# Three gate products and the neighbourhood values as seven half-size products, moved behind the global attention

## The chip, the cores and the metric

The kernel runs on one core of one Trainium2 chip. The metric is the device time of one execution in microseconds (us); the number compared is the median of a few runs of the same program. One execution was also recorded by the hardware profiler. Engines are named as in the profile: PE is TensorE (its matmuls), PEld its weight loads, DVE is VectorE, ACT is ScalarE, POOL is GpSimd, SP the engine that issues most of the DMAs. L185 means line 185 of the kernel.

## The reference

One encoder layer on 512 tokens of 2048 features, in fp32. What the change touches:

```python
proj = h @ w_in[l]                    # 2048 x 8704
qa, ka, va, qb, kb, vb, ga, gb = jnp.split(proj, offs, axis=-1)
...
ya = global_gqa(qa, ka, va)           # 8 heads, 2 key heads, all 512 keys
yb = neighbourhood_attention(qb, kb, vb, nat_rpb[l])   # 8 heads, 8 x 16 windows
merged = jax.nn.sigmoid(ga) * (ya @ w_oa[l]) + jax.nn.sigmoid(gb) * (yb @ w_ob[l])
x = x + g1 * (merged @ w_out[l])
```

Before it, `mod = SiLU(c) @ w_ada + b_ada` gives six vectors of 2048 (shift, scale and gate of the two sub-layers); behind it come an RMS norm, a SwiGLU of width 5632 and a final norm.

## The kernel before

Every product is made three times, from a high and a low half of each operand: `split` (L161 to L165) copies a tile to fp32r on ACT (hi, L163) and subtracts it from the source on DVE (lo, L165), and `mm3` (L180 to L185) issues hi times hi, hi times lo and lo times hi into the same PSUM bank. Weights come as 512 KB pieces: `unit` (L187) loads one into one of 4 `raw` buffers from SP's queue, `wsplit` (L193) splits it into one of 3 `whl` buffers. Later stages add 1 `raw` and 2 `whl` buffers from the pool `wq` (`buffer`, L131).

Two loops use them. `form1` (L230) keeps weights stationary and streams the 512 tokens: two banks of 128 output columns, four pieces, 96 matmuls of 512 columns for a contraction over 2048. `form2` (L248) keeps tokens stationary and streams 512 weight columns: four banks, eight pieces, 192 matmuls. After each piece both call `pump` (L210), which carries on background work: callbacks that are due (`soon`), one of the list `later`, and `pace["steps"]` steps of the generators in `bg`.

The stages around the change, in program order:

- Global attention, `att_a` (L701), four heads, the last four columns of gate A, four heads more (L725 to L733). Its results go to DRAM (`y_d`).
- The pool `p_w` is made and the eight generators of `ada_mod` and `ada_gate` go to `bg` (L736 to L740): 128 steps, each of which loads 512 KB of `w_ada` from POOL's queue into one of three `mw` buffers and adds it, times a column of `c`, to an accumulator on DVE (L357, L335). Four groups of 16 steps make shift2 and scale2, two make gate1, two make gate2. Gate B, columns 0 to 1023 (`gates(sg_b, GB, 0, 8)`, L741): four `form1`.
- Neighbourhood attention (L799 to L808): for each half of the heads the values by `form2` (L801), then for each pair of heads queries and keys by `form1` and two calls of `att_b` (L747): scores, softmax, transposes, values.
- Gate B, columns 1024 to 2047 (L820): four `form1`; through `later` each piece also loads one head's attention result and splits it (`attended`, L814).
- For each pair of output columns one `form1` with `w_oa` and one with `w_ob` (L853 to L857), both over 8 heads; `gated` (L840) multiplies by the sigmoid gate; sum and split give `mT` (L858 to L865). `paces` (L852) gives one or two `ada` steps for each piece.
- `w_out` (L949 to L958): columns 0 and 1 for all tokens, columns 2 and 3 for the first half, then, after a norm of that half, for the second.
- The up and gate products of the SwiGLU by `group7` (L1054): a product of 2 x 2 blocks with seven block products in place of eight (Strassen's scheme in Winograd's form). `wforms` (L998) loads two pieces, makes four sums of quarters on DVE (L1008 to L1011) and splits four tiles; `xforms` has made the same for the features. A step of 512 features is 84 matmuls of 256 columns, four steps a group; then L1080 to L1090 add the banks up.

The order of instructions on each engine is fixed when the program is built, by a list scheduler that takes the first ready instruction by program order in its own model of time; on the chip each engine runs its list in order. Matmuls of a later product so come to stand between the steps of a softmax.

Of the kernel before, what the change touches and what calls it, by code (L numbers as in the profile page):

```python
# [54 lines left out]
MERGED = stream_order(T)  # L55
LAST = MERGED[stream_order(T // 2)]
# [56 lines left out]
def encoder_block(ctx: ExitStack, tc, xp, xT, c, ada1_w, ada2_w, b_ada, norm1_w, w_in, q_norm_w, k_norm_w, bias,  # L113
# [92 lines left out]
    pace = {"steps": 1}  # L206

    paces = []

    def pump():  # L210
        if paces:
            pace["steps"] = paces.pop(0)
# [6 lines left out]
        for _ in range(pace["steps"]):  # L219
            advance()  # L220

    def advance():
        if bg:
            try:
                next(bg[0])
            except StopIteration:
                bg.pop(0)
                advance()

    def form1(ws, c0, g, xs, banks, evac, eng=V):  # L230
# [17 lines left out]
    def form2(w, c0, xs, evac, r0=0, eng=V, tiles=range(NT), tags=("mm",) * NT):  # L248
# [309 lines left out]
    for k1 in range(1, KT + 1):  # L558
# [19 lines left out]
        for c0, accs, ends in GROUPS:  # L578
# [8 lines left out]
            for i, acc in enumerate(accs):  # L587
                sl = slice(i * P, (i + 1) * P)
                b = bank(next(turn))
                for k in range(a0, k1):  # L590
# [3 lines left out]
                    else:  # L594
                        mm3(b, wh[:, sl], wl[:, sl], hh, hl, k == a0, k == k1 - 1, T)
# [17 lines left out]
    def gates(dst, base, j0, j1, eng=V):  # L613
        for j in range(j0, j1, 2):
            form1([w_in], base + j * P, 2, hT, [[bank("mm"), bank("mm")]], keep_gate(dst[j:]), eng)


    p_a = tc.alloc_tile_pool(name="p_a", bufs=1, side="right")
    behind(nc.sync.dma_start(rp, rope.rearrange("p (i s d) -> p i s d", i=NT, s=2)))
    nw = {}  # L620
    for nm, w in (("q", q_norm_w), ("k", k_norm_w)):
        nw[nm] = small.tile([P, HD], F32, tag=f"nw{nm}", name=f"nw{nm}", bufs=1)
        nc.sync.dma_start(nw[nm], w.partition_broadcast(P).rearrange("p o d -> p (o d)"))

    def head_ssq(src, nh, acc):
        for h in range(nh):
            junk = io.tile([P, 512], F32, tag="io", name="junk")[:, :HD]
            S.activation(junk, src[:, h * HD:(h + 1) * HD], AF.Square, accum_out=acc[:, h:h + 1])

    def norm_rope(src, nh, i, r, w, dst):  # L630

        n = nh * HD
        h3 = lambda a: a[:, :n].rearrange("p (h d) -> p h d", h=nh)
        bt = lambda a: a.unsqueeze(1).to_broadcast([P, nh, a.shape[1]])
        a, b, rot = (p_a.tile([P, 512], F32, tag="rt", name="rt", bufs=3) for _ in range(3))
        for h in range(nh):
            hs = slice(h * HD, (h + 1) * HD)
            V.scalar_tensor_tensor(b[:, hs], src[:, hs], r[:, h:h + 1], w, op0=ALU.mult, op1=ALU.mult)
        V.tensor_mul(h3(a), h3(b), bt(rp[:, i, 0, :]))
        for e in range(2):  # L640
            V.tensor_mul(h3(rot)[:, :, e::2], h3(b)[:, :, 1 - e::2], bt(rp[:, i, 1, e::2]))
        V.tensor_add(a[:, :n], a[:, :n], rot[:, :n])
        tp = bank("T")
        for h in range(nh):
            nc.tensor.transpose(tp[:, h * P:(h + 1) * P], a[:, h * HD:(h + 1) * HD], ident)
        hi, lo = (d.rearrange("p (h t) -> p h t", h=nh)[:, :, i * P:(i + 1) * P] for d in dst)
        split(hi, lo, h3(tp))

    kT = pair(p_a, "k", 2 * T, 1)

    def rstds(srcs, nh):
        ssq = small.tile([P, 16], F32, tag="ssq16", name="ssq16")[:, :NT * nh]
        for i, src in enumerate(srcs):
            head_ssq(src, nh, ssq[:, nh * i:nh * i + nh])
        r = rsqrt_mean(ssq, HD, NT * nh)
        return [r[:, nh * i:nh * i + nh] for i in range(NT)]

    def normed(srcs, nh, w, dst):
        rs = rstds(srcs, nh)
        for i, r in enumerate(rs):  # L660
            norm_rope(srcs[i], nh, i, r, w, dst)
            yield

    def values():
        for i in range(NT):
            v = st(F32R)
            vA.append((v[:, :256], v[:, 256:]))
            split(*vA[i], kv[i][:, 256:])
            if i % 2:
                yield  # L670

    vA = []
    q = pair(p_a, "q", 4 * T, 1)
    bg.extend([normed(kv, 2, nw["k"], kT), normed(q_acc, 4, nw["q"], q), values()])
    q1 = [st(F32) for _ in range(NT)]
    form2(w_in, QA + 512, hT, lambda i, b: S.activation(q1[i], b, AF.Copy))
    while bg or soon:
        pump()

    y_d = [dram.tile([P, T], F32, name=f"y{h}") for h in range(16)]  # L680

    def keep_y(h, yb):
        o = aside.tile([P, T], F32, tag="y", name="yo")
        S.activation(o.rearrange("p (h e i) -> p h e i", e=2, i=P), apart(yb), AF.Copy)
        nc.scalar.dma_start(y_d[h], o)

    def softmax(pool, src, scale, w, bufs=2):

        mx = small.tile([P, 1], F32, tag="mx", name="mx")
        V.reduce_max(mx, src, axis=AX.X)  # L690
        V.tensor_scalar(mx, mx, -scale, None, op0=ALU.mult)
        e = pool.tile([P, 512], F32, tag="e", name="e", bufs=bufs)[:, :w]
# [8 lines left out]
    def att_a(h, q, j, kv):  # L701
        kh, kl = (t[:, kv * T:(kv + 1) * T] for t in kT)
        vs = slice(kv * HD, (kv + 1) * HD)
        pts = []
        for i in range(NT):
            if i % 2 == 0:
                pts.append(pair(p_a, "pt", 2 * T, 3))
            sl = slice(j * T + i * P, j * T + (i + 1) * P)
            sc = bank("S")
            mm3(sc, q[0][:, sl], q[1][:, sl], kh, kl, True, True, T)  # L710
            e = softmax(p_a, sc, SCALE, T)
            tp = bank("T")
            for k in range(NT):
                nc.tensor.transpose(tp[:, k * P:(k + 1) * P], e[:, k * P:(k + 1) * P], ident)
            hi, lo = (t.rearrange("p (k q) -> p k q", k=NT)[:, :, i % 2 * P:(i % 2 + 1) * P] for t in pts[-1])
            split(hi, lo, tp.rearrange("p (k q) -> p k q", k=NT))
        yb = bank("Y")
        for n, pt in enumerate(pts):
            ys = yb[:, n * 256:(n + 1) * 256]
            for k in range(NT):  # L720
                ks = slice(k * 256, (k + 1) * 256)
                mm3(ys, vA[k][0][:, vs], vA[k][1][:, vs], pt[0][:, ks], pt[1][:, ks], k == 0, k == NT - 1, 256)
        keep_y(h, yb)

    for h in range(4):  # L725
        att_a(h, q, h, 0)
    q = pair(p_a, "q", 4 * T, 1)
    bg.append(normed(q1, 4, nw["q"], q))
    gates(sg_a, GA, 12, 16)
    while bg or soon:  # L730
        pump()
    for h in range(4):
        att_a(4 + h, q, h, 1)  # L733
    p_a.release()
    p_q.release()
    p_w = tc.alloc_tile_pool(name="p_w", bufs=1, side="right")  # L736
    mod["pool"] = p_w
# [771 lines left out]
```

## Time and profile before

| | |
|---|---|
| median of 3 runs | 2490.66 us (2487.54 to 2491.2) |
| the profiled execution | 2481.72 us, span 2480.0 us |
| granted TensorE clock in it | 0.999 |
| PE busy | 2449.8 us, 16607 matmuls |
| DVE busy | 1883.9 us |
| ACT busy | 1027.6 us |
| moved by DMA | 457.46 MB, 184 GB/s over the span |

A row of the view by windows gives, for a stretch of the span, each engine's busy time with the number of its instructions, the granted clock, the mean busy share of the 16 DMA engines and what they moved. A row of the waits names who waited, for whom, for how long in total, how many times, and the longest. A row of a tile or a line gives shortest, median and longest duration in ns and the first and last start. Matmuls are pipelined: a record of 275 ns does not mean that the next one starts 275 ns later, so the cost of a matmul is read from how many of them fit into a stretch.

### The profile page before, as it was taken

The page shows a single profiled execution, that of the slowest core. Times are in us where ns is not written, and L with a number is a line of the kernel's source. Part 1 is how long each engine was busy: PE and PEld are TensorE (multiplying, and loading weights), DVE is VectorE, ACT ScalarE, POOL GpSimd, SP SyncE. Part 2 cuts the span into 40 slices and gives each one's busy share as a digit, 9 for nine tenths or more (in the row PEclk, how much of TensorE's full clock was granted, in tenths as well). Part 3 has the DMA queues.
Part 4 walks back from the last instruction along what each step waited for, and adds up shares of the span by engine and source line. Part 5 has one row for each costly group of instructions (what it writes and reads, how often), then busy time and mean ns, then how long its engine had stood idle before and what let it go on. Part 6 is the DMA issues. An engine that isn't in the chain of part 4 may idle for free.

```text
span 2480.0 us, 40653 instructions
## 1 busy us (share of the span) xinstructions
PE 2449.8 (99%) x16607; PEld 2270.1 (92%) x16607; DVE 1883.9 (76%) x2511; ACT 1027.6 (41%) x1424; POOL 151.0 (6%) x254
## 2 busy tenths in 40 slices
PE   8999999999999999999999999999999999999998
PEld 7888888888888888888999999999999998999997
DVE  8995776556566577566898888888888885787877
ACT  5223544224334333236744444444444454434333
POOL 0100000111011111011000000000000000000010
PEclk9999999999999999999999999999999999999999
DMA  9864234865655877676353343433433456547563
GB/s 362 296 245 156 81 102 135 273 203 184 191 187 195 300 252 264 233 266 229 111 170 117 122 130 127 136 125 112 132 128 129 135 187 227 190 141 242 192 243 127
DMA packets 217466, 457.46 MB, mean 184 GB/s; under 512 B 15056, under 2 KB 68672, under 8 KB 208832
## 3 DMA queue, kind: packets, MB, share of 16 engines
q1 hardware_dynamic: 179872, 308.19, 37.6%
q0 software_dynamic: 29728, 132.20, 15.2%
q10 hardware_dynamic: 7680, 14.48, 1.6%
q8 instruction: 130, 2.13, 0.3%
q14 instruction: 56, 0.46, 0.1%
HBM read 410.74 MB, written 44.07 MB: 183 GB/s over the span
## 4 chain that ended last, share of the span: by engine, by line
PE 82%; DVE 9%; DMA 4%; issue 2%; ACT 1%; DVEq 0%; POOL 0%; ACTq 0%; POOLq 0%
PE mm L185 18%; PE mm L184 18%; PE mm L183 17%; PE S L183 6%; PE S L184 6%; PE S L185 6%; PE Y L183 3%; PE Y L184 3%; PE Y L185 3%; DVE raw L492 2%; DVE whl L165 2%; DMA raw<-in_w_down 1%; DMA yr<-y 1%; PE T L185 1%; PE T L183 1%
## 5 line engine op out<-in xcount | busy, mean ns | idle before, releaser
L163 ACT ACTIVATE whl<-raw 128x1024 fp32r<-128x1024 f32 (+1 forms) x483 | 462.0, 960 | 758.5 <-PE mm L185 376.5
L165 DVE TENSOR_TENSOR whl<-raw,whl 128x1024 fp32r<-128x1024 f32 (+1 forms) x483 | 531.2, 1109 | 255.5 <-ACT whl L163 255.1
L165 DVE TENSOR_TENSOR whl<-ta,whl 128x1024 fp32r<-128x1024 f32 x104 | 127.2, 1223 | 66.4 <-ACT whl L163 66.4
L357 DVE SCALAR_TENSOR_TENSOR acc<-mw,cact,acc 128x1024 f32<-128x1024 f32 x124 | 158.4, 1278 | 18.8 <-DMA mw<-in_ada_w 14.0
L163 ACT ACTIVATE whl<-tb 128x1024 fp32r<-128x1024 f32 x104 | 110.4, 1061 | 149.6 <-PE S L185 120.1
L163 ACT ACTIVATE whl<-ta 128x1024 fp32r<-128x1024 f32 x104 | 110.1, 1059 | 144.8 <-PE mm L185 113.9
L165 DVE TENSOR_TENSOR whl<-tb,whl 128x1024 fp32r<-128x1024 f32 x104 | 127.0, 1221 | 4.6 <-ACT whl L163 3.6
L335 POOL DMA_DIRECT2D mw<-in_ada_w x112 | 59.8, 534 | 681.7 <-DVE acc L357 384.1
L1008 DVE TENSOR_TENSOR ta<-raw 128x512 f32<-128x512 f32 x104 | 71.8, 690 | 31.5 <-DMA raw<-in_w_down 29.3
L1009 DVE TENSOR_TENSOR ta<-raw,ta 128x512 f32<-128x512 f32 x104 | 71.6, 688 | 28.0 <-DMA raw<-in_w_down 24.9
L183 PE MATMUL mm<-x56h,whl 128*128 128x256 f32 x336 | 92.4, 275 | 0.0
L184 PE MATMUL mm<-x56l,whl 128*128 128x256 f32 x336 | 92.4, 275 | 0.0
L185 PE MATMUL mm<-x56h,whl 128*128 128x256 f32 x336 | 92.4, 275 | 0.0
L183 PE MATMUL mm<-whl,s 128*128 128x256 f32 x320 | 88.1, 275 | 0.0
L183 PE MATMUL mm<-x3h,whl 128*128 128x256 f32 x320 | 88.0, 275 | 0.0
L184 PE MATMUL mm<-x3l,whl 128*128 128x256 f32 x320 | 88.0, 275 | 0.0
L185 PE MATMUL mm<-x3h,whl 128*128 128x256 f32 x320 | 88.0, 275 | 0.0
L183 PE MATMUL S<-x56h,whl 128*128 128x256 f32 x320 | 88.0, 275 | 0.0
L184 PE MATMUL S<-x56l,whl 128*128 128x256 f32 x320 | 88.0, 275 | 0.0
L185 PE MATMUL S<-x56h,whl 128*128 128x256 f32 x320 | 88.0, 275 | 0.0
L184 PE MATMUL mm<-whl,s 128*128 128x256 f32 x320 | 88.0, 275 | 0.0
L185 PE MATMUL mm<-whl,s 128*128 128x256 f32 x320 | 88.0, 275 | 0.0
(1603 smaller groups left out, 8574.4 us busy)
## 6 DMA issues: line engine op xcount, KB each, us to landing
raw<-in_w_in SPq DMA_DIRECT2D x133, 512.0 KB, 4.4
mw<-in_ada_w POOLq DMA_DIRECT2D x112, 512.0 KB, 4.9
raw<-in_w_gate SPq DMA_DIRECT2D x92, 512.0 KB, 3.6
raw<-in_w_up SPq DMA_DIRECT2D x88, 512.0 KB, 3.6
raw<-in_w_down SPq DMA_DIRECT2D x88, 512.0 KB, 5.2
raw<-in_ada_w POOLq DMA_DIRECT2D x29, 1024.0 KB, 7.0
raw<-in_w_out SPq DMA_DIRECT2D x48, 512.0 KB, 5.1
ffd<-c SPq DMA_DIRECT2D x10, 1024.0 KB, 4.8
```

The costliest lines, as they stand in the source:

```text
L163: high = pin(S.activation(hi, src, AF.Copy))
L165: latest[:] = [high, pin(eng.tensor_sub(lo, src, hi))]
L183: nc.tensor.matmul(o, lh, rh, start=start, stop=False, **kw)
L184: nc.tensor.matmul(o, lh, rl, start=False, stop=False, **kw)
L185: nc.tensor.matmul(o, ll, rh, start=False, stop=stop, **kw)
L335: mod["queue"].dma_start(w, ada2_w[n * P:(n + 1) * P, :])
L357: behind(V.scalar_tensor_tensor(acc, part, cact[:, k:k + 1], acc, op0=ALU.mult, op1=ALU.add))
L492: V.scalar_tensor_tensor(raw, raw, 1.0, call, op0=ALU.mult, op1=ALU.mult, accum_out=y)
L1008: V.tensor_sub(t1, b12, b11)
L1009: V.tensor_sub(t2_, b22, t1)
```

## The change

- Gate B's first 512 columns stay plain, right behind the global attention (two `form1`). Their `pump` calls run `FORMS`: for each 512 features, POOL adds hi and lo back to the whole feature (16 additions of 128x512), then DVE makes four sums and two splits (`feature_forms`).
- Gate B's other 1536 columns become three calls of `group7`, and the neighbourhood values two (`by_tokens`: tokens stationary). The pool `p_o` gives them 1 `raw` and 1 `whl` buffer more than the first 4 and 3. The values go to DRAM (`v_d`) and are loaded and split again per half of the heads.
- Only behind that is `p_w` made. The 128 `ada` steps (now the list `mods`) are paced by `slot`: called twice per piece of `form1` and `form2` and twice per head in `att_b`, it adds a rate (0.85 in the neighbourhood attention, 0.72 in `w_oa` and in five of the eight column groups of `w_ob`, 0.6 and 0.5 in `w_out`) and makes a step when the sum reaches 1. At most 96 steps run before `w_out`; the rest load from SP's queue there.
- Behind the last keys the global attention's results are loaded and split into the memory of the features, ahead of the last two heads. Then `w_oa` runs for all columns, its gated results stay in `oa`, and `w_ob` follows for all columns, with the neighbourhood results loaded during `w_oa` and 1 `raw` and 2 `whl` buffers more.
- Products of 512 columns stream as two blocks of 256 (`mm3(..., 256)` in place of `T`), and the host's orders of the tokens change with it.

The core of the diff (`half`, `ORDER`, `wforms` and the rest of the seven-product functions move up unchanged):

```diff
+    def slot():
+        pace["due"] += pace["rate"]
+        if pace["due"] >= 1 and (fetched or mod["next"] < mod["end"]):
+            pace["due"] -= 1
+            advance(mods)
...
-                        mm3(bs[j], hi[:, kk, sl], lo[:, kk, sl], xh, xl, k0 + kk == 0, k0 + kk == n - 1, T)
+                        mm3(bs[j], hi[:, kk, sl], lo[:, kk, sl], xh, xl, k0 + kk == 0, k0 + kk == n - 1, 256)
+                    if kk == m // 2 - 1:
+                        slot()
...
-    def group7(wsrc, xs, order, dst, first_group=False):
+    def group7(wsrc, xs, order, dst, first_group=False, by_tokens=False):
...
+                            if by_tokens:
+                                mm3(o, xh[at], xl[at], wh[:, q], wl[:, q], first, last, 256, skip_group_check=True)
+                            else:
+                                mm3(o, wh[at], wl[at], xh[:, q], xl[:, q], first, last, 256, skip_group_check=True)
+            pump()
...
+    def whole_features(s):
...
+        for k in range(4):
+            G.tensor_add(f[:, k * 512:(k + 1) * 512], *hT[4 * s + k])
+        whole.append(f)
+
+    def feature_forms(s):
...
+        V.tensor_add(sa0, a21, a22)
+        V.tensor_sub(sa1, sa0, a11)
+        V.tensor_sub(sb0, a11, a21)
+        V.tensor_sub(sb1, a12, sa1)
...
+        for src, rs in ((sa, (5, 6)), (sb, (7, 3))):
+            hl = pair(p_o[0], f"s{s}{rs[0]}", 1024, 1)
+            split(*hl, src)
...
+    FORMS = [None, None, wf(0), wf(1), ff(0), wf(2), ff(1), ff(2), wf(3), ff(3)]
+    later.extend(f or (lambda: None) for f in FORMS)
+    gates(sg_b, GB, 0, 4)
+    wq = p_o[0]
+    more_buffers(1, 1)
...
+        group7(lambda s: wforms(w_in, 4 * s, GB + n * 512), hs, range(4), dst)
+        S.activation(c[0], c[0], AF.Sigmoid)
...
+        group7(lambda s: wforms(w_in, 4 * s, VB + hh * 512), hs, range(4), lambda: d, by_tokens=True)
+        nc.scalar.dma_start(v_d[hh], v)
...
+    for n in range(1, 4):
+        gates7(n)
+    for hh in range(2):
+        values7(hh)
...
-    mod["pool"] = p_w
-    bg.extend(ada_mod(k, (s2, b_sc2, n2, t2, b_sh2)) for k in range(0, KT, 4))
+    mod.update(pool=p_w, end=96)
+    mods.extend(ada_mod(k, (s2, b_sc2, n2, t2, b_sh2)) for k in range(0, KT, 4))
...
-    gates(sg_b, GB, 0, 8)
...
-        form2(w_in, VB + half * 512, hT, lambda i, b: split(*v[i], b))
...
+        if hp == 3:
+            p_h.release()
+            p_m = tc.alloc_tile_pool(name="p_m", bufs=1, side="left")
...
+            for h in range(8):
+                attended(ya[h], h, raw_tile("yr")[:, :T])
+        for j in range(2):
+            att_b(h0 + j, qs[j], ks[j], v, slice((hp % 2 * 2 + j) * HD, (hp % 2 * 2 + j + 1) * HD))
...
-    gates(sg_b, GB, 8, KT)
...
+    for j in range(0, KT, 2):
+        tag = next(turn)
+        form1([w_oa], j * P, 2, ya, [[bank(tag), bank(tag)]], gated(sg_a[j:], lambda e: oa[j // 2][:, e * 512:(e + 1) * 512]))
...
+        form1([w_ob], j * P, 2, yT, [[bank(tag), bank(tag)]], gated(sg_b[j:], lambda e: o[e]))
```

More of the change, by code (lines that the diff above doesn't have):

```diff
@@ L611, in keep_gate, with gates @@
         return evac
-    def gates(dst, base, j0, j1, eng=V):
+    def gates(dst, base, j0, j1):
         for j in range(j0, j1, 2):
[L615 to L680, printed above, removed]
@@ L701, in att_a @@
[L701 to L736, printed above, removed]
-    mod["pool"] = p_w
-    bg.extend(ada_mod(k, (s2, b_sc2, n2, t2, b_sh2)) for k in range(0, KT, 4))
-    g1_d, g2_d = ([dram.tile([1, 512], F32, name=f"g{n}d{q}") for q in range(4)] for n in (1, 2))
@@ L866, in encoder_block @@
-    p_y.release()
-    p_w.release()
-    aside.release()
-    taken.update({t: -1 - taken[t] for t in ("raw", "whl")})
-    wq = tc.alloc_tile_pool(name="wq", bufs=1, side="right", reuse_waits="tile")
-    x2_d = dram.tile([T, D], F32, name="x2d")
-    p_w = tc.alloc_tile_pool(name="p_w2", bufs=1, side="left", reuse_waits="tile")
-    mod.update(pool=p_w, queue=nc.sync, end=128)
-    p_r = tc.alloc_tile_pool(name="p_r", bufs=1, side="right", reuse_waits="tile")
-    gate = p_r.tile([P, D], F32, name="gate1")
@@ new lines, in values @@
+    def values():
+        for i in range(NT):
+            v = st(F32R)
+            vA.append((v[:, :256], v[:, 256:]))
+            split(*vA[i], kv[i][:, 256:])
+            if i % 2:
+                yield
+    vA = []
+    q = pair(p_a, "q", 4 * T, 1)
+    bg.extend([normed(kv, 2, nw["k"], kT), normed(q_acc, 4, nw["q"], q), values()])
+    q1 = [st(F32) for _ in range(NT)]
+    form2(w_in, QA + 512, hT, lambda i, b: S.activation(q1[i], b, AF.Copy))
+    flush()
+    y_d = [dram.tile([P, T], F32, name=f"y{h}") for h in range(16)]
@@ new lines, in encoder_block, with __init__, __getitem__ @@
+    for h in range(4):
+        att_a(h, q, h, 0)
+    q = pair(p_a, "q", 4 * T, 1)
+    bg.append(normed(q1, 4, nw["q"], q))
+    gates(sg_a, GA, 12, 16)
+    flush()
+    for h in range(4):
+        att_a(4 + h, q, h, 1)
+    p_a.release()
+    p_q.release()
+    p_o = []
+    quarters = lambda t: t.rearrange("p (a t q n) -> p a t q n", a=2, t=2, q=2)
+    class Cut:
+        def __init__(self, tiles, t):
+            self.tiles, self.t0 = tiles, t * 256
+        def __getitem__(self, ix):
+            c = ix[2] if len(ix) > 2 else slice(0, 256)
+            return self.tiles[ix[1]][:, self.t0 + c.start:self.t0 + c.stop]
@@ new lines, in encoder_block @@
+    for j in range(0, KT, 2):
+        pace["rate"] = 0.72 if j < 10 else 0.0
+        o = [p_y.tile([P, T], F32, tag="o", name="o", bufs=4) for _ in range(2)]
+        tag = next(turn)
+        form1([w_ob], j * P, 2, yT, [[bank(tag), bank(tag)]], gated(sg_b[j:], lambda e: o[e]))
+        for e in range(2):
+            V.tensor_add(o[e], o[e], oa[j // 2][:, e * 512:(e + 1) * 512])
+        mx.append(pair(p_m, f"m{j // 2}", 1024, 1))
+        for e in range(2):
+            mT.append(tuple(Tokens(half(t)[:, :, e]) for t in mx[-1]))
+            (mh, ml), o3 = (t.t for t in mT[-1]), o[e].rearrange("p (t n) -> p t n", t=2)
+            if j + 2 < KT:
+                split(mh, ml, o3)
+            else:
+                V.tensor_copy(mh, o3)
+                V.tensor_sub(ml, o3, mh)
@@ new lines, in encoder_block @@
+    wq = None
+    p_y.release()
+    p_w.release()
+    aside.release()
+    more_buffers(1, 2)
+    wq = tc.alloc_tile_pool(name="wq", bufs=1, side="right", reuse_waits="tile")
+    x2_d = dram.tile([T, D], F32, name="x2d")
+    p_w = tc.alloc_tile_pool(name="p_w2", bufs=1, side="left", reuse_waits="tile")
+    mod.update(pool=p_w, queue=nc.sync, end=128)
+    p_r = tc.alloc_tile_pool(name="p_r", bufs=1, side="right", reuse_waits="tile")
+    gate = p_r.tile([P, D], F32, name="gate1")
+    xc = {cc: p_r.tile([P, NT, 512], F32, tag=f"x{cc}", name=f"x{cc}") for cc in (3, 2)}
@@ new lines, in encoder_block, with load_x @@
+    xn = [None, None, xc[2], p_r.tile([P, NT, 512], F32, tag="n3", name="n3")]
+    xc.update({cc: p_r.tile([P, NT, 512], F32, tag=f"x{cc}", name=f"x{cc}") for cc in (0, 1)})
+    xn[:2] = xc[0], xc[1]
+    sq2 = [small.tile([P, 4], F32, tag=f"sq{i}", name=f"sq{i}", bufs=1) for i in range(NT)]
+    x3d = xp.rearrange("(i p) d -> p i d", p=P)
+    def load_x(cc):
+        if cc == 0:
+            rows(gate, g1_d)
+        nc.sync.dma_start(xc[cc], x3d[:, :, cc * 512:(cc + 1) * 512])
+    for cc in range(4):
+        later.extend([lambda: None] * (2 if cc == 0 else 3))
+        later.append(functools.partial(load_x, cc))
```

514 lines of the change are left out of this document (299 added, 215 removed).

## The prediction

> **What bounds the kernel now.** First the page: who is busy, and who ends the chain of waits.
>
> ```profile
> span 2480.0 us, 40653 instructions
> ...
> PE 2449.8 (99%) x16607; PEld 2270.1 (92%) x16607; DVE 1883.9 (76%) x2511; ACT 1027.6 (41%) x1424; POOL 151.0 (6%) x254
> ...
> PE 82%; DVE 9%; DMA 4%; issue 2%; ACT 1%; DVEq 0%; POOL 0%; ACTq 0%; POOLq 0%
> ```
>
> TensorE is busy nearly throughout. Next, windows by stage: gate B's first half, neighbourhood attention, gate B's second half, `w_oa` with `w_ob`, three stretches of `w_out`; last, 600 us of `group7`. Columns: stretch, its length, busy us (instructions) of PE, PEld, DVE, ACT, POOL, clock, DMA share, GB/s.
>
> ```profile
> 413.00:496.00 83.00, 82.68 (x384) 71.99 (x383) 42.19 (x36) 23.04 (x26) 11.78 (x23) 1.00 0.85 282
> 496.00:778.00 282.00, 280.90 (x1398) 240.84 (x1397) 174.57 (x250) 103.14 (x194) 32.70 (x58) 1.00 0.56 179
> 778.00:861.00 83.00, 81.31 (x375) 70.19 (x374) 53.90 (x57) 31.64 (x42) 14.12 (x25) 1.00 0.92 314
> 861.00:1026.00 165.00, 165.00 (x766) 144.33 (x765) 117.16 (x136) 48.72 (x60) 18.93 (x35) 1.00 0.71 242
> 1026.00:1109.00 83.00, 83.00 (x386) 72.66 (x385) 49.52 (x46) 24.47 (x34) 12.87 (x12) 1.00 0.81 280
> 1109.00:1150.00 41.00, 41.00 (x192) 35.76 (x191) 25.13 (x25) 19.62 (x26) 8.06 (x6) 1.00 0.71 230
> 1300.00:1900.00 600.00, 600.00 (x5375) 600.00 (x5375) 515.50 (x640) 264.98 (x281) 0.00 (x0) 1.00 0.39 127
> ```
>
> Two prices follow. Between 861 and 1026 all matmuls have 512 columns: 165/766 = 215.4 ns each. From 1300 to 1900 all have 256: 600/5375 = 111.6 ns. Streaming in blocks of 512 (first row) or of 256 (fifth) gives the same 215 ns, so `T` to 256 costs nothing. What PE waited for between 395 and 1200 us:
>
> ```profile
> PE mm L185 <- DVE whl L165: 1.9, 3, 0.9
> PE T L778 <- ACT e L770: 1.0, 3, 0.3
> ```
>
> So there is hardly a wait to remove. The change must win by fewer matmuls, and loses whatever new waits it makes.
>
> **The product saving.** Five products of 512 tokens, 512 columns and 2048 features change. Plain: 16 x 4 x 3 = 192 matmuls of 512 columns, 192 x 215.4 = 41.4 us. Sevenfold: 4 steps x 84 = 336 of 256 columns, 336 x 111.6 = 37.5 us. Saved 3.9 us each, 5 x 3.86 = **19.3 us**. It is not an eighth (5.2 us), because two half matmuls cost 223 ns where one whole costs 215: about 8 ns of each matmul do not shrink with its columns.
>
> [...] In `group7` weight loads are busy 600 of 600 us and the spacing is still 111.6 ns, so they are hidden, just. [...]
>
> **The old stall.** The second half of gate B (778 to 861) loses 1.7 us of PE time, the 1.9 us of the wait above, while 16 attention results arrive at 314 GB/s. That crowd goes: **-1.9 us**.
>
> **DVE in the five groups.** 1300 to 1900 holds 64 steps; DVE works 515.5/64 = 8.05 us of each 9.37, with sums, splits, bank additions and products in it. PE lost nothing there. The new groups have one `whl` buffer less, four for the four tiles of a step, so a tile is refilled in the place it had one step before. Its cost by rows of one refill: ACT's copy, DVE's subtraction, and first use.
>
> ```profile
> 1374.00 1.06 ACT L163 ACTIVATE whl<-ta 128x1024 fp32r<-128x1024 f32 x1 [1.67 <-PE mm L185]
> 1375.09 1.23 DVE L165 TENSOR_TENSOR whl<-ta,whl 128x1024 fp32r<-128x1024 f32 x1 [1.50 <-ACT whl L163]
> ...
> 1383.13 0.28 PE L183 MATMUL mm<-x56h,whl 128*128 128x256 f32 x1
> ```
>
> The tile is ready at 1376.3 and used at 1383.1: 6.8 us spare. Without the fifth buffer it starts one tile later, 24 x 111.6 = 2.7 us, so 4 us are left. Seven bank additions at a group's end (0.6 us each, 4.2) can just eat that. I take **+1 us** for all five boundaries, from 0 (as in the row) to 6.
>
> The feature forms add, per 512 features, four sums and two splits. By the page's groups (690 and 1221 ns): 4 x 0.69 + 2 x 1.22 = 5.2 us of DVE. Three sets lie in gate B's plain 41 us, where DVE had 21 us of work, half of it `ada` steps that leave. The fourth lies in the first group: 4 x 8.05 + 5.2 = 37.4 of 37.5 us. And POOL's 16 additions disturb DVE:
>
> ```profile
> L899 POOL TENSOR_TENSOR x<-x,ro x14: 1269/1281/2332, 1061.8 to 1192.1; 128x512 f32<-128x512 f32 x14
> ...
> 1071.13 2.25 POOL L899 TENSOR_TENSOR x<-x,ro 128x512 f32<-128x512 f32 x1 [5.27 <-DVE ro L898]
> ...
> 1072.16 2.30 DVE L165 TENSOR_TENSOR whl<-raw,whl 128x1024 fp32r<-128x1024 f32 x1
> 1074.38 1.27 DVE L357 SCALAR_TENSOR_TENSOR acc<-mw,cact,acc 128x1024 f32<-128x1024 f32 x1
> 1075.58 1.21 DVE L165 TENSOR_TENSOR whl<-raw,whl 128x1024 fp32r<-128x1024 f32 x1
> ```
>
> The split beside the POOL addition took 2.30 us, alone 1.21. Four of the 16 fall into the first group: up to 4.4 us of DVE. The three split tiles ahead of PE hide part: **+1.5 us**, 0 to 4. [...]
>
> **Edits at nothing.** The values now go to DRAM and back: 4 MB of DMA, with the splits that they had before. Queries and keys of the first pair, 41 us, lie between store and use; uncovered it would be one landing of a piece:
>
> ```profile
> raw<-in_w_in SPq DMA_DIRECT2D x133, 512.0 KB, 4.4
> ```
>
> ACT copies four tiles a step and has 265 of 600 us of work in the last window, so the sigmoids and stores of the new groups find room. The host's new orders of the tokens change addresses only.
>
> **The last pair of heads.** Rows of such a pair, from the keys' copy to the last result:
>
> ```profile
> 756.99 1.25 ACT L163 ACTIVATE kh<-mm 128x512 fp32r<-128x512 f32 x2 [2.96 <-PE mm L185]
> ...
> 764.34 0.41 PE L778 MATMUL T<-ident,e 128*128 128x128 f32 x2 [0.32 <-ACT e L770]
> ...
> 772.41 0.60 PE L778 MATMUL T<-ident,e 128*128 128x128 f32 x4
> ...
> L787 ACT ACTIVATE yo<-Y x16: 323/372/438, 577.5 to 776.0; 128x320 f32<-128x320 f32 x8, 128x192 f32<-128x192 f32 x8
> ```
>
> It lasts 757 to 776, 19 us, of which PE's own work is 48 x 0.112 + 16 x 0.15 = 7.8 us; the other 11 were filled with gate B's matmuls, ready at any time. Behind the change the filling is `w_oa`, which needs the attention's results split into memory that the last keys free. A split is short:
>
> ```profile
> L163 ACT ACTIVATE y0h<-yr x1: 631/631/631, 776.3 to 776.3; 128x512 fp32r<-128x512 f32 x1
> ...
> L165 DVE TENSOR_TENSOR y0l<-yr,y0h x1: 694/694/694, 776.9 to 776.9; 128x512 fp32r<-128x512 f32 x1
> ```
>
> The first can follow the two key copies, about 2.6 us behind the last key matmul, and one is due every 1.3 us after (6 matmuls of 215 ns). On SP's queue the eight loads stand behind the last key weights and wait for a `raw` buffer only. PE has scores to do in between: **+2 us**, from 0 to 11 (no filling at all).
>
> **The `ada` steps.** They start behind the five groups in place of ahead of gate B, so the same 128 steps have less time. 96 stay on POOL's queue, where nothing else waits behind them but small stores; 32 in place of 16 go to SP's.
>
> ```profile
> L357 DVE SCALAR_TENSOR_TENSOR acc<-mw,cact,acc 128x1024 f32<-128x1024 f32 x124 | 158.4, 1278 | 18.8 <-DMA mw<-in_ada_w 14.0
> ...
> L335 SPq DMA_DIRECT2D mw<-in_ada_w x16: 327/340/1108, 1021.0 to 1080.3; - x16
> ```
>
> Counting `slot` calls: 60 steps in the neighbourhood attention, 23 in `w_oa`, 13 in `w_ob`, 20 in `w_out` columns 0 and 1, 12 in the first half of columns 2 and 3. DVE (1.28 us a step) has room everywhere but in the last, where a step and a split (1.22) take 2.5 of the 2.6 us of 12 matmuls. DMA is tighter. In `w_oa`: 16 weight pieces and 23 steps (0.52 MB each), 16 gates and 8 results (0.26 MB): 26.8 MB in 83 us, 323 GB/s. The nearest row is 778 to 861 with 314 GB/s, which cost 1.9 us: **+1.9**, 0 to 4. In `w_out` 16 more steps come to the 83 x 280 + 41 x 230 = 32.7 MB of the rows: 41.1 MB in 124 us, 331 GB/s, most of it in the second part. Five weight buffers lie ahead there: **+1**, 0 to 10. A step that waits for its load holds DVE and with it the splits behind it; SP's queue holds the next weights behind a step whose buffer is not free.
>
> **Sum.** -19.3 - 1.9 + 1 + 1.5 + 2 + 1.9 + 1 = -13.8 us: span 2466.2, own time 2481.7 - 13.8 = 2467.9. The profiled execution lies 8.9 us under the median 2490.66, so the median becomes **2476.9**. About 0.2% (5 us) is what a measurement can tell from no change.
>
> **Rivals.**
> - *Loads become the bound* from `w_oa` to `w_out`. If long stretches hold no more than the 314 GB/s of the busiest row, `w_oa` takes 26.8/0.314 = 85.4 us (+2.6) and `w_out` 41.1/0.314 = 130.9 (+6.9): 9.5 in place of 2.9, 2483.5; with DVE held behind late steps a few more, 2486. For it: share 0.92 already at 314. Against: `mw` waits cost DVE 14 us and PE nothing. 7%.
> - *The last pair is not filled*: +11 in place of 2, 2485.9. For it: the schedule has nothing else there. Against: the short splits. 7%.
> - *Slower: four buffers are too few.* If DVE's fixed order puts one split ahead of the one PE needs, each of the 20 steps waits 1.22 us: 24.4 in place of 1, +9.6, 2500.3. It decides from (13.8 + 1)/20 = 0.74 us a step. For it: DVE 86% busy. Against: 4 us spare. 11%.
> - [...] The last window excludes it: 1%.
>
> The forecast, 74%, has its own range 2468 to 2484. The whole range reaches to the first two rivals, 2468 to 2487. Faster 0.74; the first two rivals, about -5 us, are the 0.14 within 0.2%; slower 0.12.
>
> **What would show it.** Right: 5 x 336 matmuls spaced 111.6 ns, DVE near 85% in these 188 us, PE waits under 3 us in them; a gap of 1 to 3 us behind the last keys; 300 GB/s or more in `w_oa` with PE losing about 2 us. Wrong: PE waiting for `whl` in every step; idle PE of 5 us or more between the last keys and `w_oa`; DMA share at 0.95 with PE waits in `w_out`.

## The result and the profile after

The change makes the kernel slower. After: 2529.95 us median of 4 runs (2527.98 to 2530.78); before, on the same chip: 2489.1 us (2483.69 to 2491.2). The ratio is 1.0166, with a 95% interval from 1.0148 to 1.0185. The forecast was 2476.9. The profiled execution took 2529.71 us (span 2527.9, mean granted clock 0.991), the one before 2481.72 (clock 0.999): 48.0 us more. By the medians it is 40.9, as the profiled execution before lies 7 us below its median.

The lines of the kernel after: L167 and L169 are the two halves of `split`, L187 to L189 the three matmuls of `mm3`, L351 and L373 load and add an `ada` step, L390 is its row product, L908 is POOL's addition, L918 to L921 are the sums of the feature forms. In the edited kernels of the experiments the numbers lie a few lines further on.

First the page: busy time, and the engines in the chain that ended last.

```profile
span 2527.9 us, 42439 instructions
...
PE 2448.4 (97%) x17327; PEld 2285.7 (90%) x17327; DVE 2022.3 (80%) x2690; ACT 1073.6 (42%) x1470; POOL 169.8 (7%) x254
...
PE 65%; DVE 13%; issue 9%; DMA 9%; ACT 2%; POOL 1%; DVEq 0%; POOLq 0%; SPq 0%; ACTq 0%
```

PE's share of the chain fell from 82% to 65%. PE no longer paces the kernel everywhere: the shares of DVE, DMA and issue rose. Windows by stage say where: feature forms, the five seven-product groups, neighbourhood attention, its last pair of heads, `w_oa` with the first half of `w_ob`, the rest of `w_ob`, `w_out`. Columns as in the prediction.

```profile
413.00:470.00 57.00, 46.34 (x277) 41.41 (x276) 50.97 (x49) 23.61 (x27) 25.93 (x16) 0.91 0.30 88
470.00:640.00 170.00, 170.00 (x1523) 169.97 (x1522) 139.53 (x173) 76.74 (x80) 0.00 (x0) 1.00 0.46 140
640.00:840.00 200.00, 189.19 (x947) 160.94 (x946) 151.07 (x206) 76.55 (x147) 35.25 (x64) 1.00 0.77 255
840.00:860.00 20.00, 9.57 (x54) 7.90 (x52) 13.24 (x26) 11.19 (x23) 3.36 (x6) 0.92 0.75 252
860.00:1010.00 150.00, 141.35 (x634) 119.94 (x633) 122.26 (x151) 52.34 (x75) 28.41 (x50) 0.95 0.85 293
1010.00:1060.00 50.00, 50.00 (x234) 43.70 (x233) 30.09 (x41) 13.38 (x17) 3.26 (x5) 1.00 0.44 149
1060.00:1180.00 120.00, 109.72 (x484) 93.96 (x483) 83.07 (x74) 36.50 (x50) 18.61 (x16) 0.94 0.87 302
...
880.00:900.00 20.00, 20.00 (x94) 17.48 (x93) 14.56 (x15) 7.74 (x13) 4.12 (x8) 1.00 1.01 368
1140.00:1160.00 20.00, 17.94 (x74) 14.82 (x73) 18.08 (x18) 8.02 (x14) 7.05 (x6) 0.91 0.99 365
```

The seven-product groups do what was forecast: 170 us without a gap, 170.00/1523 = 111.6 ns a matmul. (The start of the first group, with gaps of 2.2 and 1.7 us, lies in the row above.) The loss is around them. PE is idle for 10.7 us in the first row, 10.8 in the third, 10.4, 8.7 and 10.3 in the fourth, fifth and seventh: 50.8 us, against 3.1 in the prediction's rows for 413 to 1026. Three numbers close the sum: 47.7 us more idle time, 19.3 less matmul work, and a granted clock of 0.991 in place of 0.999, which over 2528 us is 20: 47.7 - 19.3 + 20 = 48.4, measured 48.0. PE's busy time says the same of the clock: it fell by 1.4 us (2449.8 to 2448.4) where 19.3 less work was due.

What PE waited for, in the view of waits:

```profile
PE mm L189 <- DVE whl L169: 12.9, 6, 6.8
PE mm L187 <- ACT whl L167: 9.1, 2, 8.2
PE T L1008 <- DVE e L1005: 6.2, 2, 5.9
...
PE S L188 <- DVE kl L169: 4.6, 3, 3.5
PE T L390 <- DVE accl L169: 4.1, 3, 2.1
...
PE Y L390 <- DVE ada_o L394: 2.6, 1, 2.6
```

In this part of the kernel PE waits for splits and softmax results, not for a load itself. It also waits for the `ada` sums directly: their row products (L390) are matmuls at a fixed place in PE's order, and stand when a sum is late. All waits at these products and for the PSUM bank that one holds come to 10.6 us between 395 and 1200; in `steps_no_loads` below they are 2.0. Each wait is read back one step further in the timeline.

**The feature forms.** DVE's and, in the second fence, POOL's timeline (start, duration, in brackets the idle time before and what ended it).

```profile
411.44 1.23 DVE L169 TENSOR_TENSOR whl<-raw,whl 128x1024 fp32r<-128x1024 f32 x1 [0.42 <-ACT whl L167]
415.19 1.74 DVE L920 TENSOR_TENSOR sb<-hc 128x512 f32<-128x512 f32 x1 [2.53 <-POOL hc L908]
418.10 1.75 DVE L918 TENSOR_TENSOR sa<-hc 128x512 f32<-128x512 f32 x1 [1.16 <-POOL hc L908]
...
433.66 1.22 DVE L169 TENSOR_TENSOR whl<-raw,whl 128x1024 fp32r<-128x1024 f32 x1
```

```profile
412.65 1.27 POOL L908 TENSOR_TENSOR hc<-h0h,h0l 128x512 f32<-128x512 f32 x1 [252.15 <-DVE whl L169]
...
427.24 2.24 POOL L908 TENSOR_TENSOR hc<-h10h,h10l 128x512 f32<-128x512 f32 x1
```

Between 411.44 and 433.66 DVE splits no weight. Its fixed order has the sums of three sets of features first, they wait for POOL, and beside POOL's additions a sum takes 1.75 us where the prediction had 0.69. The next weight split stands behind all of them, and PE runs dry at 428.

**Neighbourhood attention and `w_oa`.** DVE's waits between 640 and 1200, then its timeline ahead of a stall.

```profile
DVE acc L373 <- DMA mw<-in_ada_w: 36.8, 30, 3.2
```

```profile
732.33 1.28 DVE L373 SCALAR_TENSOR_TENSOR acc<-mw,cact,acc 128x1024 f32<-128x1024 f32 x1 [1.20 <-DMA mw<-in_ada_w]
733.53 1.22 DVE L169 TENSOR_TENSOR whl<-raw,whl 128x1024 fp32r<-128x1024 f32 x1
734.66 0.68 DVE L169 TENSOR_TENSOR kl<-mm,kh 128x512 fp32r<-128x512 f32 x1
```

A step that waits for its load holds whatever is behind it on DVE. Here that is a weight split and then `kl`, for which PE's score products wait (3.50 us, until 735.40). The order alone does not do it: the kernel before had 43 steps in its neighbourhood attention, at 179 GB/s, and DVE waited for none of their loads. After, between 640 and 840, at 255 GB/s, it waited at 17 of 51 steps, 16.7 us in all; of PE's 10.8 us there, 4.1 stand at the row products or their bank and 4.4 at `kl`.

**The last pair of heads.** ACT's timeline:

```profile
845.45 0.63 ACT L1076 ACTIVATE g<-g 128x512 f32<-128x512 f32 x1 [8.14 <-DMA g<-sga]
...
854.24 1.26 ACT L167 ACTIVATE ya<-yr 128x512 fp32r<-128x512 f32 x2 [1.19 <-DMA yr<-y]
855.52 1.28 ACT L1000 ACT_TABLE_LOAD   x1
856.82 0.52 ACT L1000 ACTIVATE e<-sb,mx 128x256 f32<-128x256 f32 x1
```

ACT stands 8.14 us on the load of a gate (about 1 us of it counts, as PE works on the keys until 844.6), then copies eight attention results, some late, and only then comes the first exponential.

**The start of `w_out`.** SP's queue, and ACT's copy behind it:

```profile
1045.67 0.43 SPq L1128 DMA_DIRECT2D x<-in_xp  x1
1059.24 12.25 SPq L351 DMA_DIRECT2D mw<-in_ada_w  x6
1071.54 0.59 SPq L194 DMA_DIRECT2D raw<-in_w_out  x1
...
1078.23 1.06 ACT L167 ACTIVATE whl<-raw 128x1024 fp32r<-128x1024 f32 x1 [16.29 <-DMA raw<-in_w_out]
```

From 1045.67 to 1071.54 SP issues nothing but six `ada` loads, whose buffers come free late; the next piece of `w_out` stands behind them. Between 1060 and 1200 ACT waits 44.7 us for weights of `w_out` (13.6 in the kernel before), DVE only 2.8 for the `ada` loads, so here the delay reaches PE by way of the weights. PE's timeline there also shows the clock:

```profile
1070.78 0.38 PE L189 MATMUL S<-whl,m3l 128*128 128x512 f32 x1
1079.34 1.22 PE L187 MATMUL mm<-whl,m4h 128*128 128x512 f32 x2 [8.18 <-ACT whl L167]
...
1082.04 0.63 PE L189 MATMUL mm<-whl,m4l 128*128 128x512 f32 x1
1082.47 0.63 PE L187 MATMUL S<-whl,m4h 128*128 128x512 f32 x1
...
1084.60 0.63 PE L189 MATMUL S<-whl,m4l 128*128 128x512 f32 x1
```

Behind the gap matmuls of 512 columns start 0.43 us apart, twice the 0.215 of the prediction's first price. The granted clock is 0.50 from 1079 to 1085. The slow stretch lasts at least 5.3 us (1079.34 to 1084.60). Behind a wait of 1.83 us stand some 3 us of such matmuls (from 1153.74), behind the wait of 3.50 us that ended at 735.40 none (clock 1.00 from 720 to 740). What starts and ends such a stretch these rows do not show.

```profile
1153.11 0.50 PE L390 MATMUL T<-accl,ones_r 128*128 128x512 f32 x1 [1.83 <-DVE accl L169]
...
1155.02 0.63 PE L188 MATMUL mm<-whl,m2h 128*128 128x512 f32 x1
1155.45 0.63 PE L189 MATMUL mm<-whl,m2l 128*128 128x512 f32 x1
```

### The profile page after: what moved, and what is told of

It reads as the page before. It is cut to its first block, busy times and chain, and to the rows that moved or that the text cites. A ratio compares the mean times of both kernels' runs of the same rounds, so it can differ in the third digit from the quotient of the medians.

```text
span 2527.9 us, 42439 instructions
## 1 busy us (share of the span) xinstructions
PE 2448.4 (97%) x17327; PEld 2285.7 (90%) x17327; DVE 2022.3 (80%) x2690; ACT 1073.6 (42%) x1470; POOL 169.8 (7%) x254
## 4 chain that ended last, share of the span: by engine, by line
PE 65%; DVE 13%; issue 9%; DMA 9%; ACT 2%; POOL 1%; DVEq 0%; POOLq 0%; SPq 0%; ACTq 0%
PE mm L189 13%; PE mm L187 13%; PE mm L188 13%; PE S L187 5%; PE S L189 5%; PE S L188 5%; DMA mw<-in_ada_w 4%; DVE whl L169 3%; DMA raw<-in_w_down 3%; PE Y L187 2%; PE Y L188 2%; PE Y L189 2%; DVE raw L508 2%; DVE acc L373 1%; DMA yr<-y 1%
## 5 line engine op out<-in xcount | busy, mean ns | idle before, releaser
L167 ACT ACTIVATE whl<-raw 128x1024 fp32r<-128x1024 f32 (+1 forms) x483 | 453.6, 942 | 666.0 <-PE mm L189 253.5
L169 DVE TENSOR_TENSOR whl<-raw,whl 128x1024 fp32r<-128x1024 f32 (+1 forms) x483 | 519.7, 1087 | 133.4 <-ACT whl L167 132.8
L169 DVE TENSOR_TENSOR whl<-ta,whl 128x1024 fp32r<-128x1024 f32 x124 | 151.6, 1223 | 78.6 <-ACT whl L167 78.6
L167 ACT ACTIVATE whl<-tb 128x1024 fp32r<-128x1024 f32 x124 | 131.5, 1061 | 183.8 <-PE S L189 121.8
L167 ACT ACTIVATE whl<-ta 128x1024 fp32r<-128x1024 f32 x124 | 131.3, 1059 | 170.6 <-PE mm L189 110.6
L373 DVE SCALAR_TENSOR_TENSOR acc<-mw,cact,acc 128x1024 f32<-128x1024 f32 x124 | 158.6, 1279 | 37.6 <-DMA mw<-in_ada_w 36.8
L169 DVE TENSOR_TENSOR whl<-tb,whl 128x1024 fp32r<-128x1024 f32 x124 | 151.3, 1220 | 8.6 <-ACT whl L167 7.1
L679 DVE TENSOR_TENSOR ta<-raw,ta 128x512 f32<-128x512 f32 x124 | 86.4, 697 | 33.7 <-DMA raw<-in_w_down 27.8
L678 DVE TENSOR_TENSOR ta<-raw 128x512 f32<-128x512 f32 x124 | 85.5, 690 | 32.1 <-DMA raw<-in_w_down 29.5
L187 PE MATMUL mm<-x56h,whl 128*128 128x256 f32 x336 | 92.4, 275 | 0.0
L189 PE MATMUL mm<-x56h,whl 128*128 128x256 f32 x336 | 92.4, 275 | 0.0
L187 PE MATMUL mm<-whl,s 128*128 128x256 f32 x320 | 88.1, 275 | 0.0
L680 DVE TENSOR_TENSOR tb<-raw 128x512 f32<-128x512 f32 x124 | 86.3, 696 | 2.1 <-DMA raw<-in_w_down 0.2
L187 PE MATMUL mm<-x3h,whl 128*128 128x256 f32 x320 | 88.0, 275 | 0.0
L189 PE MATMUL mm<-x3h,whl 128*128 128x256 f32 x320 | 88.0, 275 | 0.0
L187 PE MATMUL S<-x56h,whl 128*128 128x256 f32 x320 | 88.0, 275 | 0.0
L189 PE MATMUL S<-x56h,whl 128*128 128x256 f32 x320 | 88.0, 275 | 0.0
L189 PE MATMUL mm<-whl,s 128*128 128x256 f32 x320 | 88.0, 275 | 0.0
```

The source lines that it names most:

```text
L167: high = pin(S.activation(hi, src, AF.Copy))
L169: latest[:] = [high, pin(eng.tensor_sub(lo, src, hi))]
L187: nc.tensor.matmul(o, lh, rh, start=start, stop=False, **kw)
L189: nc.tensor.matmul(o, ll, rh, start=False, stop=stop, **kw)
L373: behind(V.scalar_tensor_tensor(acc, part, cact[:, k:k + 1], acc, op0=ALU.mult, op1=ALU.add))
L678: V.tensor_sub(t1, b12, b11)
```

## The experiments

Theory A: the `ada` loads are the main loss. They come in less time, land late, and DVE and SP's queue, each in its fixed order, hand the delay on to splits and weights. Theory B: what costs is DVE's own work for the steps, or the seven-product form. Two smaller places were to be separated: POOL's additions and the last pair. Every kernel is compared with runs of the kernel before on its own chip; the ratio is to these, with its 95% interval.

**`few_steps`**: 15 of each 16 steps left out, loads and DVE work, in the kernel after. **`few_steps_before`**: the same edit in the kernel before.

```diff
-            fetch()
-            part = fetched.popleft()
+            mod["steps"] = mod.get("steps", 0) + 1
+            if k == 0:
+                fetch()
+                part = fetched.popleft()
...
-            else:
+            elif k == 0:
```

> The changed kernel with one load and one multiply-add in place of 16 for each of the eight modulation rows (15 of 16 ada steps left out; the row sums and everything else stay). Theory: the 128 steps, pressed together behind the five seven-product groups, cost the waits at 720 to 830 us (about 10), 900 to 990 (10), 1070 (8) and 1150 (2), with some us of lowered clock behind them: 2530 - 35 = 2495 us. Rival: the steps are hidden and the feature forms and the last pair of heads cost it all: 2520 or more.

> The kernel before with the same 15 of 16 ada steps left out. Theory: there they lay beside products with room, so nearly nothing is gained: 2485 to 2488 us against 2489. Rival: the steps cost as much before as after: 2455 us. The difference of this pair is the change without its steps: by the theory -19 for the products, +14 for the feature forms and +14 for the last pair of heads.

Measured: 2489.3 us in the kernel after, ratio 1.0012 (1.0002 to 1.0022), and 2481.29 in the kernel before, 0.9987 (0.9978 to 0.9996). The steps cost some 40 us in the kernel after and 3 in the kernel before. Even without them the change is 8 us behind (6 by the ratios), so there is a second loss.

**`steps_no_loads`**: all steps on DVE, but three loads per pool (there are two, so 6 loads in place of 128).

```diff
-            w = mod["pool"].tile([P, 1024], F32, tag="mw", name="mw", bufs=3)
-            mod["queue"].dma_start(w, ada2_w[n * P:(n + 1) * P, :])
-            fetched.append(w)
+            kept = mod.setdefault(id(mod["pool"]), [])
+            if len(kept) < 3:
...
+            fetched.append(kept[n % 3])
```

> The changed kernel with all ada steps on DVE but only three loads per pool: later steps reuse the three tiles (125 of 128 loads left out in effect). If the loads are the cause (DMA at 0.95 to 1.0 of its time, DVE and SP's queue waiting for them): 2500 to 2505 us, almost the gain of leaving the steps out. If DVE's own time in the steps is the cause: 2522 or more.

**`steps_short`**: all loads, but DVE's step over 64 of 1024 columns.

```diff
-                behind(V.scalar_tensor_tensor(acc, part, cact[:, k:k + 1], acc, op0=ALU.mult, op1=ALU.add))
+                behind(V.scalar_tensor_tensor(acc[:, :64], part[:, :64], cact[:, k:k + 1], acc[:, :64], op0=ALU.mult, op1=ALU.add))
```

> The changed kernel with all 128 loads but a multiply-add over 64 of 1024 columns (about 0.15 in place of 1.28 us each; the rest of the sum is left out). If the loads are the cause: 2520 or more. If DVE's own time is: 2500 to 2505 us.

Measured: 2488.21, ratio 1.0017 (1.0008 to 1.0026), without the loads; 2519.33, 1.0136 (1.0119 to 1.0153), with the loads and hardly any DVE work. Without loads the steps are free (2488.2 against 2489.3 with hardly a step). In the profiled executions, 42.0 us apart, PE is idle for 31.4 us less without the loads and busy for 10.6 us less with the same matmuls, at a granted clock of 0.994 against 0.991. Windows of `steps_no_loads`, neighbourhood attention and `w_oa`:

```profile
640.00:840.00 200.00, 196.13 (x986) 167.42 (x985) 157.44 (x217) 81.34 (x156) 8.28 (x13) 1.00 0.38 123
...
860.00:1010.00 150.00, 150.00 (x708) 131.25 (x707) 125.61 (x151) 54.72 (x71) 8.58 (x13) 1.00 0.54 176
```

DVE did more work there than in the kernel after (157 against 151 us, 126 against 122), and PE lost 3.9 (most of it where the last pair begins) and 0 in place of 10.8 and 8.7. In `steps_short` DVE waits even longer for the loads:

```profile
DVE acc L373 <- DMA mw<-in_ada_w: 72.1, 42, 5.2
```

So it is mainly the waits, not the work: some 31 of the 40 us stay. What the short step saves, 7 us by the ratios and 11 by the medians, it saves only where late loads have made DVE late.

**`act_whole`** and **`dve_whole`**: POOL's 16 additions replaced by ACT's copies of the high halves, or made on DVE.

```diff
-            G.tensor_add(f[:, k * 512:(k + 1) * 512], *hT[4 * s + k])
+            V.tensor_add(f[:, k * 512:(k + 1) * 512], *hT[4 * s + k])
```

> The changed kernel with POOL's 16 additions (hi + lo) replaced by 16 ACT copies of hi; the low halves are left out of the feature sums. Theory: DVE lost the time at 412 to 450 us waiting for POOL's additions and being stretched beside them (1.75 for 0.69 us); 11 us of waits and 4 of clock go: 2516 us. Rival: DVE has too much to do there in any case: 2528 or more.

> The changed kernel with the 16 additions on DVE instead of POOL (nothing left out). Theory: 16 x 0.6 = 10 us more work for DVE but no wait for POOL and no stretched operations (about 12 us): of the 15 us some 5 to 10 come back: 2522 us. Rival: DVE's load alone is the cause there, then it gets worse: 2535 us.

Measured: 2517.12, ratio 1.0127 (1.0109 to 1.0145), and 2519.1, 1.0134 (1.0119 to 1.015). A window of `dve_whole`:

```profile
413.00:470.00 57.00, 55.15 (x378) 51.28 (x377) 56.54 (x76) 28.54 (x32) 0.00 (x0) 1.00 0.40 123
```

DVE is busy for 56.5 of 57 us, and yet PE loses 1.9 us where POOL's help cost it 10.7. Moving the additions to DVE saves 8 us (by the ratios) to 11 (by the medians), though DVE is then full. Some of the kernels below start from `dve_whole`; where they do, it is said.

**`pool_queue`**: the last 32 `ada` loads from POOL's queue. **`w_out_late`** (from `dve_whole`): the first step in `w_out` two pieces later.

```diff
-    mod.update(pool=p_w, queue=nc.sync, end=128)
+    mod.update(pool=p_w, queue=nc.gpsimd, end=128)
```

```diff
-        later.extend([lambda: None] * (2 if cc == 0 else 3))
+        later.extend([lambda: None] + [lambda: pace.update(rate=0.75)] if cc == 0 else [lambda: None] * 3)
...
-    pace["rate"] = 0.6
+    pace["rate"] = 0.0
```

> The changed kernel, with the last 32 ada loads issued from POOL's queue instead of SP's. Theory: the wait of 8.4 us at 1070 us comes from SP's queue, which stood from 1046 to 1071 behind loads whose buffers were not free and held the weights of w_out; with the lowered clock behind it 8 to 12 us go: 2519 us. Rival: the DMA engines were simply full there: 2528 or more.

> A complete kernel: the additions on DVE, and in w_out the first ada step comes two weight pieces later, so that the first weights of w_out are ahead of its ada loads on SP's queue; the 32 steps then follow at a rate of 0.75 in place of 0.6. If the wait of 8 us at the start of w_out is made by the ada loads that stand in SP's queue for their buffers, it goes, and most of it stays gone: about 2511 (2519 less 8). If it is the rate of the transfers that limits w_out, the same loads come in a shorter stretch and the loss returns behind it: 2517 to 2521.

Measured: 2523.29, ratio 1.0152 (1.0122 to 1.0182), and 2521.9, 1.0129 (1.0111 to 1.0147), against 1.0134 of `dve_whole`. Windows over `w_out`, of `dve_whole` and of `w_out_late`:

```profile
1060.00:1180.00 120.00, 108.75 (x490) 93.16 (x489) 80.81 (x72) 38.54 (x52) 17.16 (x13) 0.96 0.89 309
```

```profile
1060.00:1180.00 120.00, 107.96 (x475) 91.92 (x474) 82.14 (x74) 41.52 (x57) 23.02 (x14) 0.96 0.84 285
```

The one wait of 8.6 us at the start became four between 0.8 and 4.6 us; PE loses 12.0 in place of 11.3. So in this pair the order in SP's queue chooses the place of the wait, not its size. My expectation of 2511 fell. In `pool_queue` PE loses 7.6 us over the same stretch (10.3 in the kernel after), and the time lies between what the theory (2519) and its rival (2528) say; its runs spread over 15 us, so it decides nothing.

**`gate_behind`**: gate B's last 512 columns plain again, as filling behind the last pair.

```diff
-    for n in range(1, 4):
+    for n in range(1, 3):
         gates7(n)
...
+        for j in range(2):
+            att_b(h0 + j, qs[j], ks[j], v, slice((hp % 2 * 2 + j) * HD, (hp % 2 * 2 + j + 1) * HD))
         if hp == 3:
+            pace["rate"] = 0.0
+            gates(sg_b, GB, 12, KT)
```

> The changed kernel with gate B's last 512 columns plain again and placed behind the last pair of heads, ahead of the loads of the global attention's results (no ada steps in them). Theory: the last pair then has matmuls to fill its softmax, as before: 14 us come back (11 of waits, 3 of clock), 3.9 are lost on the plain product and about 3 on waiting for the first attention result afterwards: 2523 us. Rival: the waits of the last pair come from ACT and DVE being late, not from missing filling: 2531 or more.

Measured: 2530.88, ratio 1.0184 (1.0169 to 1.02). The number is the rival's, the reason another. The softmax is filled, but the wait stands behind the gate: PE now stands 11.1 us, with nothing beside it, for the attention results, which go into the memory that gate B frees, and then for the first weights of `w_oa`, whose loads stand behind them on SP's queue. A window of `gate_behind`:

```profile
860.00:880.00 20.00, 8.84 (x29) 6.59 (x28) 12.22 (x16) 8.94 (x13) 1.06 (x2) 0.66 0.74 249
```

**`dve_no_loads`**: `dve_whole` with the edit of `steps_no_loads`, to see whether the two losses add up.

> The kernel after with two of its new burdens gone: the 16 additions that make the whole features run on DVE, and of the loads of the ada weights only three per pool are made (the steps multiply old data, so shift, scale and both gates are wrong). If three things explain the loss, namely loads, POOL additions and the last pair of heads, the first two add up: steps_no_loads measured 2488.2 and the additions on DVE saved about 11 us, so 2477, below the kernel before by about 9 us, with some 8 us of PE gaps left in the last pair and clock 0.998 or more. If the two overlap (the gaps of one hide those of the other), 2484 or more. Against the kernel before without these steps (2481.3 to 2484.6) the product saving of 19 us should then be visible less the last pair's 8 to 10.

Measured: 2479.18, ratio 0.996 (0.9947 to 0.9974): below the kernel before. Windows of `dve_no_loads` by stage:

```profile
413.00:470.00 57.00, 55.14 (x373) 50.99 (x373) 55.81 (x74) 29.11 (x33) 0.00 (x0) 1.00 0.39 117
640.00:820.00 180.00, 179.18 (x902) 152.73 (x902) 148.14 (x202) 76.33 (x147) 5.92 (x10) 1.00 0.39 123
820.00:840.00 20.00, 9.84 (x55) 8.51 (x55) 11.00 (x23) 10.26 (x21) 1.46 (x2) 0.91 0.46 148
840.00:990.00 150.00, 149.75 (x704) 130.16 (x703) 131.03 (x162) 58.30 (x82) 8.60 (x13) 0.99 0.56 175
990.00:1150.00 160.00, 157.96 (x729) 137.20 (x728) 114.95 (x118) 53.53 (x73) 25.90 (x24) 1.00 0.58 195
```

The two add up, as near as the runs can tell: loads 2519.1 - 2479.2 = 40 us (43 by the ratios; 37 with the additions on POOL), POOL's additions 8 to 11 with the loads and 9 (by the ratios 14) without. What is left of idle time is 15.1 us, 10.2 of it in the last pair. With the forecast saving the sum closes again: -19.3 + 15.1 - 3.1 + 5 (clock 0.997 against 0.999) = -2.3, and the profiled execution, 2479.65, is 2.1 below the one before (on its own chip's medians it is 8.8 below). PE is busy for 2433.7 us, 16.1 less than before at a slightly lower clock. So the seven-product form does save about 19 us.

**`half_ahead_no_loads`** and **`half_ahead`** (from `dve_no_loads` and `dve_whole`): four of the eight attention results split behind the first head's exponentials.

```diff
-            for h in range(8):
+            for h in range(4):
                 attended(ya[h], h, raw_tile("yr")[:, :T])
...
+            if hp == 3 and j == 0:
+                with tc.issue_after(exps[-1]):
+                    for h in range(4, 8):
+                        attended(ya[h], h, raw_tile("yr")[:, :T])
```

> As dve_no_loads (additions on DVE, of the ada weights only three loads per pool, so shift, scale and both gates are wrong), and of the eight attention results that are split ahead of the last two heads only four stand ahead; the other four are held until the first head's exponentials are issued on ACT. In dve_no_loads TensorE stood 3.1 and 7.3 us there while ACT made eight copies in its fixed order, some late with their loads, ahead of the exponentials. If the order on ACT and DVE is what the last pair costs, the two gaps of 10.4 us fall to 5 to 7 and the time by 3 to 6, to about 2475. If it is the memory that only the last keys free, or the softmax's own chain, the gaps stay near 10 and the time at 2479.

> The same order of the splits with all loads: a complete kernel, with the additions on DVE. By the first theory 2514 to 2516 (2519 less 3 to 5); the loads then still cost some 35 us. By the second 2519, as dve_whole measured.

Measured: 2479.4, ratio 0.9981 (0.9971 to 0.9991), and 2515.76, 1.0125 (1.0104 to 1.0146). The first exponential on ACT, in `dve_no_loads` and in `half_ahead_no_loads`:

```profile
837.32 0.52 ACT L1003 ACTIVATE e<-sb,mx 128x256 f32<-128x256 f32 x1
```

```profile
831.26 0.53 ACT L1005 ACTIVATE e<-sb,mx 128x256 f32<-128x256 f32 x1 [2.33 <-DVE mx L1002]
...
838.78 1.06 ACT L167 ACTIVATE whl<-raw 128x1024 fp32r<-128x1024 f32 x1 [0.29 <-DMA raw<-in_w_oa]
```

It comes 6 us earlier, but the weights of `w_oa` are split at 838.78 at the earliest, and PE's waits mostly moved: 3.0, 1.2, 2.5, 2.0 and 0.9 us, 8.6 together, where they were 3.0 and 7.1. The theory of the order fell, as the time did not. In the profile two chains run side by side, the softmax's and the one that readies `w_oa`, and neither has matmuls ready for the other; both orders cost the same. What would free the last pair stays open.

No complete kernel here beats the kernel before. The nearest, `half_ahead`, `w_out_late` and `dve_whole`, are 1.2 to 1.3% behind it.

## Why the prediction was wrong

- **The product saving**: -19.3, right. The spacing in the groups is 111.6 ns, and two sums close with it. Whether the 8 ns that do not shrink are a fixed cost of a matmul or the pace of the weight loads (PEld is busy for 169.97 of 170 us there) no run separates.
- **DVE in the five groups, four buffers**: +1, right; no gap from 470 to 640; the two in the first group, 3.9 us, come with the feature forms' work and shrink to 1.9 in `dve_whole`. The rival of too few buffers fell with it.
- **The feature forms and POOL**: +1.5 (0 to 4), measured 8 to 11. The prediction counted DVE's work against DVE's room (41 us with 21 of work) and found it to fit. It did fit, but in a fixed order, behind 16 additions on another engine. And the additions stretch DVE's work: in the trace an addition of 1.27 us alone takes up to 2.27 beside DVE's work, a sum 1.75 in place of 0.69; eleven operations of DVE are stretched by 11.5 us together, and it waits 6.0 us more for the additions.
- **The `ada` steps**: the step that failed. The prediction priced them by mean rates, `w_oa` +1.9 and `w_out` +1, and at nothing in the neighbourhood attention, because "`mw` waits cost DVE 14 us and PE nothing". They cost 40 us in place of 2.9, and 10.8 us of idle PE lie in the neighbourhood attention, where the term was nothing. The quoted row came from a kernel with its loads at 179 GB/s there. The rival that loads become the bound came nearest to the mechanism, at 2486: it too took bytes over rate. (A slip in it: 85.4 - 83 is 2.4, not 2.6.) The kernel before moves 234 GB/s over 413 to 1150 (the prediction's rows, weighted by length); the change takes 140 GB/s for 170 us of that and so 252 to 302 in the stages with steps. There DVE waits for a load 30 times, 1.2 us on average and 3.2 at most, and the timelines show such a lateness handed on in fixed order by DVE, by SP's queue, and by PE's own row products. From 1010 to 1060 hardly a step runs: 149 GB/s, and PE loses nothing. This room went unused, and no run tried it.
- **The old stall** (778 to 861, -1.9) went; a crowd of loads stood there at 314 GB/s with hardly a loss, and the prediction took that row as the price of dense loads. It was the wrong row: gate B's products beside it needed none of the attention results that made up the crowd. In the neighbourhood attention and `w_oa` the steps stand in one line on DVE with splits that are due at once.
- **The last pair**: +2 (0 to 11), measured 10 of idle time and some clock. The measured value lies near the upper end; the choice was wrong. The splits are as short as priced, but their loads, the gate's load and the first weights of `w_oa` are in line too.
- **The clock** had no term. Idle time of 48 us came with 20 us of slower clock (0.991 against 0.999).

The signs named ahead read: "idle PE of 5 us or more between the last keys and `w_oa`" was seen, and so was a DMA share of 0.95 and more with PE waits in `w_out` (1140 to 1160).

What stays open: how the 40 us of the loads divide between late landing and late buffers, and between DVE's order, the weights' own delay and the row products. That the loads cost it is shown by leaving them out; the ways by which they do are read from the timelines, as no run kept the loads and freed the instructions behind them. Nor did any run move the loads into the seven-product groups, which move only 140 GB/s.

## What to carry to other kernels

Price a moved stream of loads by what stands behind its consumer on that engine's fixed order, not by bytes over rate; here DVE waited 1.20 us for a load (732.33), `kl` stood two instructions behind it, and TensorE waited 3.50 us for `kl` (735.40). When a stage gets denser in work and loses its share of the loads, look at which stages must take them, and whether these have filling that needs nothing. And add the clock: behind a stall of TensorE matmuls of 512 columns started 0.43 us apart in place of 0.215, and 48 us more idle time came with some 20 us of slower clock.

## What was not expected of the hardware

- TensorE at half clock behind a wait: 0.43 us a matmul against 0.215, granted clock 0.50 (1079 to 1085), and even behind a wait of 1.83 us (1153.11), though not behind every longer one (3.50 us at 735.40).
- Both sides lost where POOL and DVE added tiles side by side (414 to 450): POOL took up to 2.27 us in place of 1.27, DVE 1.75 in place of 0.69. Moving POOL's work onto the fuller engine was faster by 8 to 11 us.
- The DMA engines at a share of 1.01 moved 368 GB/s (880 to 900), and PE lost nothing in that very window; its 8.7 us between 860 and 1010 lie outside it.
